# Seven Strassen products in fewer PSUM banks: sums kept in PSUM, copied out by ScalarE on the way

## The chip, the cores and the metric

The kernel runs on one core of one Trainium2 chip. The metric is the device time of one execution in microseconds (us); the time before is the median of three runs. A trace of one profiled execution shows every instruction of the five engines: PE is TensorE's matmul, PEld its weight load, DVE is VectorE, ACT is ScalarE, POOL is GpSimd, and SP issues most of the transfers.

## The reference

One layer of an encoder on 512 tokens with a model width of 2048, in float32. After an RMS norm one input projection makes, for each of three branches (A, B, C) with four heads of 128 columns, the columns q, k, v and a gate, and besides them three merge gates of 2048 columns. The branches are three kinds of attention. Their outputs are projected up, weighted by the sigmoid of the merge gates, added, and sent through one output projection:

```python
hn = rmsnorm(x, norm_g)
proj = jnp.einsum('bsd,dc->bsc', hn, w_in)
...
up = jnp.einsum('bsnw,nwd->bsnd', ys, w_up)
merged = jnp.sum(gates * up, axis=2)
return x + jnp.einsum('bsd,de->bse', merged, w_out)
```

## The kernel before

**Precision.** Every large product is made from three matmuls in the type float32r: an operand is split into a rounded high part and a remainder, and `mm3` (L100) adds high by high, high by low and low by high in one PSUM tile. The split of a weight tile (`split_to`, L91) is one ACT copy to `wh` and one DVE subtraction to `wl`, 128x1024 elements each.

**Products.** The input projection and the output projection take two column tiles of 128 columns at a time (`pair_task`, L298). Both operands are halved: the weights by the two halves of the model dimension, the tokens into a left half (`LH`, 256 tokens) and a right half (`RH`). Strassen's scheme in Winograd's form then needs seven products instead of eight. Each product is a *unit* (`Unit`, L124): 8 k tiles of three matmuls, so 24 matmuls of 128x256, after which `after_of` (L337) brings the product out of PSUM. With c1 and c2 the two column tiles, the results are

```
c1.L = P1 + P2            U2 = P1 + P6        U3 = U2 + P7
c2.L = U3 - P4            c2.R = U3 + P5      c1.R = U2 + P5 + P3
```

Before the change each product has a PSUM tile of its own from a ring of four (`acc`, L77, and the pool `pa`, L59), and the sums are made in SBUF: ACT copies P1 (L347), and seven DVE additions follow (L349 for P2, L351 for P6, L355 for P7, L359 for P4, L363 and L364 for P5, L368 for P3). The order of the products is 1, 2, 6, 7, 4, 5, 3. There are 54 pairs: 46 in the input projection and 8 in the output projection. The first pair of the output projection has `late=True` and another order (1, 2, 5, 3, 6, 7, 4), since its operands are only just being made. In the seven other pairs of the output projection `before_last` (`rest`, L796) adds the residual input while the last product is still running.

**Order of the work.** `units` is one list: the first head's plain column tiles (`col_task`), then pairs. A head of branch C, B or A takes four pairs: q and k, a pair of merge gates, v and gate, a pair of merge gates (the last head has its two gate pairs at the end). The work of its attention is hung between the units by offsets (`OFF`, L870, and `at`). After the input projection come the up projections (`up_units`, L719) and the output projection. While a unit runs, the weights of the two units after it are split (`LA`; `wh` and `wl` have three buffers each), so the ACT split of a unit waits until PE is done with the unit three before it.

**Who decides the order on an engine.** The program is written in order, and the framework's planner gives each engine its final list by simulating the program: the earliest written instruction that is ready in its simulation goes next. PE's own order is held fixed to the written one for the first 17 units only (L850 to L854); after that the planner may put a later unit's matmuls ahead of an earlier one's. Temporary tiles of 128x512 (`t2`, L68) come from one pool of 21 buffers. They hold the norms and scores of the attention as well as a pair's `u`, `c1` and `c2`. The planner hands the buffers out in the order in which the tiles' first writes are written in the program, so the first write of a pair's `u` (the copy of P1) is listed behind every earlier written first write of such a tile.

## Time and profile before

| | before |
|---|---|
| median of 3 runs | 1399.99 us (1399.92 to 1400.05) |
| profiled execution, first to last instruction | 1397.6 us |
| mean granted TensorE clock | 0.995 |
| busy: PE, PEld | 1366.3 us, 1316.7 us |
| busy: DVE, ACT, POOL | 1191.8 us, 729.7 us, 53.7 us |

The profiled execution has no time beside its span; the runs' median is 2.4 us above that span, which is what lies before the first and after the last instruction. Matmuls are pipelined: a 128x256 matmul is shown as about 0.28 us long while the next one starts 0.12 us after it, so PE's busy time says where PE had work, and the distance of two starts says how fast it went. In a row of the timeline stand the start, the length, engine and line, the operation, output and inputs; in square brackets stands the engine's idle time before it and what ended that.

### The profile page before, as it was taken

Reading aid. Unit: us, or ns where it says so; the run is one execution under the profiler, and the core shown is the slowest. Engines: PE = TensorE matmul, PEld = TensorE weight load, DVE = VectorE, ACT = ScalarE, POOL = GpSimd, SP = SyncE. Lnnn points to the kernel's source line nnn. Section 1 sums busy time; section 2 is a strip of 40 time slices with the busy share of each in tenths; the row PEclk is TensorE's granted clock in tenths of the full one; section 3 lists DMA queues with packets and bytes.
Section 4 is the critical chain, followed back from the end, with each engine's and each line's share of the span. In section 5 each row is a group of like instructions: output and inputs, shape, how many; then the busy total and the mean of one; then the engine's idle time right before and its main releaser. Section 6 shows DMA issues by size and latency. Waiting matters only on the chain.

```text
span 1397.6 us, 25474 instructions
## 1 busy us (share of the span) xinstructions
PE 1366.3 (98%) x10452; PEld 1316.7 (94%) x10452; DVE 1191.8 (85%) x1671; ACT 729.7 (52%) x1042; POOL 53.7 (4%) x60
## 2 busy tenths in 40 slices
PE   6969999999999999999999999999999999999999
PEld 3759999999999999999999999999999988899999
DVE  8999898887978889888888888888888888898886
ACT  6345564544545555555556555545555755453332
POOL 4730000000000000000000000000000000000000
PEclk9989999999999999999999999999999999999999
DMA  7113334323344244342433333333233766535542
GB/s 272 46 46 106 122 102 126 121 91 114 106 129 126 95 114 128 113 129 95 117 122 115 121 94 119 113 114 121 91 115 103 273 197 203 169 109 176 164 151 76
DMA packets 63093, 176.39 MB, mean 126 GB/s; under 512 B 7400, under 2 KB 9320, under 8 KB 62976
## 3 DMA queue, kind: packets, MB, share of 16 engines
q1 hardware_dynamic: 59520, 170.49, 38.4%
q10 hardware_dynamic: 3456, 4.26, 0.8%
q8 instruction: 82, 1.34, 0.4%
q14 instruction: 35, 0.29, 0.1%
HBM read 155.04 MB, written 19.69 MB: 125 GB/s over the span
## 4 chain that ended last, share of the span: by engine, by line
PE 92%; DVE 5%; issue 1%; ACT 0%; POOL 0%; DMA 0%; SPq 0%; DVEq 0%; ACTq 0%; POOLq 0%
PE acc L101 27%; PE acc L103 27%; PE acc L102 27%; PE att L103 3%; PE att L101 3%; PE att L102 3%; DVE x L255 1%; DVE wl L93 1%; PE att L548 1%; PE att L517 1%; PE att L570 1%; DVE x1l L93 1%; PE att L571 1%; PE att L569 1%; DVE t23l L93 0%
## 5 line engine op out<-in xcount | busy, mean ns | idle before, releaser
L92 ACT ACTIVATE wh<-raw 128x1024 fp32r<-128x1024 f32 (+1 forms) x418 | 435.7, 1043 | 549.2 <-PE acc L102 488.2
L93 DVE TENSOR_TENSOR wl<-raw,wh 128x1024 fp32r<-128x1024 f32 (+1 forms) x418 | 503.9, 1206 | 96.7 <-ACT wh L92 95.9
L102 PE MATMUL acc<-x1l,wh 128*128 128x256 f32 (+1 forms) x768 | 222.3, 289 | 10.5 <-DVE x1l L93 10.5
L103 PE MATMUL acc<-x1h,wl 128*128 128x256 f32 (+1 forms) x768 | 222.0, 289 | 2.2 <-DVE wl L93 2.2
L101 PE MATMUL acc<-x1h,wh 128*128 128x256 f32 (+1 forms) x768 | 223.7, 291 | 0.0
L101 PE MATMUL acc<-x2h,wh 128*128 128x256 f32 (+1 forms) x768 | 223.6, 291 | 0.0
L102 PE MATMUL acc<-x2l,wh 128*128 128x256 f32 (+1 forms) x768 | 221.9, 289 | 0.9 <-DVE x2l L93 0.9
L103 PE MATMUL acc<-x2h,wl 128*128 128x256 f32 (+1 forms) x768 | 221.8, 289 | 0.0
L101 PE MATMUL acc<-t23h,wh 128*128 128x256 f32 x736 | 209.7, 285 | 0.0
L103 PE MATMUL acc<-t23h,wl 128*128 128x256 f32 x736 | 208.4, 284 | 0.0
L102 PE MATMUL acc<-t23l,wh 128*128 128x256 f32 x736 | 208.1, 283 | 0.0
L102 PEld LDWEIGHTS acc<-x1l,wh 128*128 128x128 f32 x768 | 147.8, 192 | 13.4 <-DVE x1l L93 11.2
L103 PEld LDWEIGHTS acc<-x1h,wl 128*128 128x128 f32 x768 | 147.8, 193 | 3.9 <-DVE wl L93 2.4
L102 PEld LDWEIGHTS acc<-x2l,wh 128*128 128x128 f32 x768 | 148.0, 193 | 2.4 <-DVE x2l L93 1.1
L101 PEld LDWEIGHTS acc<-x1h,wh 128*128 128x128 f32 x768 | 147.9, 193 | 1.8 <-issue 0.2
L101 PEld LDWEIGHTS acc<-x2h,wh 128*128 128x128 f32 x768 | 148.2, 193 | 1.3
L103 PEld LDWEIGHTS acc<-x2h,wl 128*128 128x128 f32 x768 | 148.0, 193 | 1.3
L101 PEld LDWEIGHTS acc<-t23h,wh 128*128 128x128 f32 x736 | 141.0, 192 | 0.5
L102 PEld LDWEIGHTS acc<-t23l,wh 128*128 128x128 f32 x736 | 141.0, 192 | 0.1
L103 PEld LDWEIGHTS acc<-t23h,wl 128*128 128x128 f32 x736 | 140.7, 191 | 0.3
L101 PE MATMUL acc<-t,wh 128*128 128x256 f32 x368 | 105.1, 286 | 0.0
L102 PE MATMUL acc<-t,wh 128*128 128x256 f32 x368 | 104.4, 284 | 0.0
(256 smaller groups left out, 2728.0 us busy)
## 6 DMA issues: line engine op xcount, KB each, us to landing
raw<-in_w_col SPq DMA_DIRECT2D x192, 512.0 KB, 3.6
raw<-in_w_out SPq DMA_DIRECT2D x32, 512.0 KB, 3.8
gl<-c SPq DMA_DIRECT2D x48, 256.0 KB, 2.0
raw<-in_w_up SPq DMA_DIRECT2D x32, 384.0 KB, 3.2
sg<-gl SPq DMA_DIRECT2D x48, 256.0 KB, 5.0
x<-in_xT SPq DMA_DIRECT2D x16, 256.0 KB, 5.4
xr<-in_xT SPq DMA_DIRECT2D x16, 256.0 KB, 4.4
yd<-y SPq DMA_DIRECT2D x11, 256.0 KB, 2.0
```

What stands on the lines that cost most here:

```text
L92: nc.scalar.activation(hi, src, AF.Copy)
L93: nc.vector.tensor_sub(lo, src, f(hi))
L101: nc.tensor.matmul(ps, lh, rh, start=start, stop=False)
L102: nc.tensor.matmul(ps, lh, rl, start=False, stop=False)
L103: nc.tensor.matmul(ps, ll, rh, start=False, stop=stop)
L255: nc.vector.scalar_tensor_tensor(x, x, gn[:, kt:kt + 1], rstd[0], op0=ALU.mult, op1=ALU.mult)
L517: nc.tensor.transpose(ps[:, blk(i)], st["p"][i][:, blk(j)], identf)
L548: nc.tensor.matmul(ps[:, i * P:], nu_r if i == j else nones_r, part, start=i == j and part is st["lk"][j][0], stop=False)
L569: nc.tensor.matmul(o, vh[:, blk(j)], st["h"][j], start=j == 0, stop=False)
L570: nc.tensor.matmul(o, vl[:, blk(j)], st["h"][j], start=False, stop=False)
L571: nc.tensor.matmul(o, vh[:, blk(j)], st["l"][j], start=False, stop=j == QB - 1)
```

## The change

Products are now accumulated onto each other in PSUM. A pair uses three tiles: bank 0 takes P1, P6, P7 and P4 on top of each other, bank 2 takes P5 and P3, bank 1 takes P2. Between two products of a bank the sum so far is copied or read: ACT copies P1, then U2 = P1 + P6, then P5; DVE adds U3 (standing in bank 0) to c2.R and U2 to what stands in bank 2. P4 enters with the other sign, for which the fourth operand is formed the other way round (`combos`, `merged_combos`), so that the last sum in bank 0 is c2.L itself and ACT copies it out. The order of the products is 1, 2, 6, 5, 7, 3, 4. The late pair keeps its order and its additions.

The PSUM ring of four becomes two buffers for bank 0 and one each for banks 1 and 2; the plain column tiles of the first head and the up projections take tiles from the same three. In the output projection the residual is added to c1 and to the right half of c2 after P3, and the left half of c2 is made by one DVE addition of the residual onto bank 0 after P4, so the last store is c2's left half instead of c1's right half. Per pair of the input projection there are three DVE additions instead of seven and four ACT copies instead of one; a pair of the output projection has three ACT copies.

```diff
-    def acc():
-        return pa.tile([P, S], F32, tag="acc", name=nm("acc"))
+    def acc(i=0):
+        return pa.tile([P, S], F32, tag=f"acc{i}", name=nm("acc"), bufs=1 if i else 2)
...
-    def mm3(ps, lh, ll, rh, rl, start, stop):
+    def mm3(ps, lh, ll, rh, rl, start, stop, more=False):
+        nc.tensor.matmul(ps, lh, rh, start=start, stop=False, skip_group_check=more)
...
-        nc.gpsimd.tensor_sub(u[:, LH], t[:, LH], b[:, LH])
+        nc.gpsimd.tensor_sub(u[:, LH], b[:, LH], t[:, LH])
...
-        order = (1, 2, 5, 3, 6, 7, 4) if late else (1, 2, 6, 7, 4, 5, 3)
+        order = (1, 2, 5, 3, 6, 7, 4) if late else (1, 2, 6, 5, 7, 3, 4)
...
         def mms_of(i):
+            p = order[i]
+            bank = i % 4 if late else {2: 1, 5: 2, 3: 2}.get(p, 0)
+            more = not late and p in (6, 7, 4, 3)
+
             def go(u):
-                st["ps"] = ps = acc()[:, LH]
+                if not more:
+                    st[bank % 3] = acc(bank % 3)[:, LH]
+                st["ps", p] = ps = st[bank % 3]
                 for j in range(UK):
-                    mm3(ps, u.hi[:, j, :], u.lo[:, j, :], *ops[order[i]](j), j == 0, j == UK - 1)
+                    mm3(ps, u.hi[:, j, :], u.lo[:, j, :], *ops[p](j), j == 0 and not more, j == UK - 1, more)
             return go
...
                 if p == 1:
                     nc.scalar.activation(u[:, LH], ps, AF.Copy)
                 elif p == 2:
                     add(c1[:, LH], u[:, LH], ps)
+                elif p == 5:
+                    nc.scalar.activation(c2[:, RH], ps, AF.Copy)
+                elif not late:
+                    if p == 6:
+                        nc.scalar.activation(u[:, RH], ps, AF.Copy)
+                    elif p == 7:
+                        add(c2[:, RH], c2[:, RH], ps)
+                    elif p == 3:
+                        add(c1[:, RH], u[:, RH], ps)
+                    elif before_last is not None:
+                        add(c2[:, LH], st["r"][:, LH], ps)
+                    else:
+                        nc.scalar.activation(c2[:, LH], ps, AF.Copy)
...
-        c = {r: col_task(col(n, r, h), xs, scaled(st, r)) for r in (Q, K, V, G)}
+        c = {r: col_task(col(n, r, h), xs, scaled(st, r), max(0, r - 1)) for r in (Q, K, V, G)}
...
-        nc.vector.tensor_sub(u, t[:, LH], b[:, LH])
+        nc.vector.tensor_sub(u, b[:, LH], t[:, LH])
...
-        def rest(c1l, c1r, c2, e=e):
-            for c, i, sl in ((c2, 1, slice(0, S)), (c1l, 0, LH), (c1r, 0, RH)):
-                if i == 1 or sl is LH:
-                    r = t2("xr")
-                    nc.sync.dma_start(r, xT[e + i])
+        def rest(c1, c2r, e=e):
+            for c, i, sl in ((c1, 0, slice(0, S)), (c2r, 1, RH)):
+                r = t2("xr")
+                nc.sync.dma_start(r, xT[e + i])
                 nc.vector.tensor_add(c, c, r[:, sl])
-            nc.scalar.dma_start(out[e + 1], c2)
-            nc.scalar.dma_start(out[e][:, LH], c1l)
+            nc.scalar.dma_start(out[e], c1)
+            nc.scalar.dma_start(out[e + 1][:, RH], c2r)
+            return r
...
-            nc.scalar.dma_start(out[e][:, RH], c1[:, RH])
+            nc.scalar.dma_start(out[e + 1][:, LH], c2[:, LH])
```

More of the change, by code (lines that the diff above doesn't have):

```diff
@@ L98, in split @@
         return hi, lo
-    def mm3(ps, lh, ll, rh, rl, start, stop):
-        nc.tensor.matmul(ps, lh, rh, start=start, stop=False)
-        nc.tensor.matmul(ps, lh, rl, start=False, stop=False)
-        nc.tensor.matmul(ps, ll, rh, start=False, stop=stop)
+    def mm3(ps, lh, ll, rh, rl, start, stop, more=False):
+        nc.tensor.matmul(ps, lh, rh, start=start, stop=False, skip_group_check=more)
+        nc.tensor.matmul(ps, lh, rl, start=False, stop=False, skip_group_check=more)
+        nc.tensor.matmul(ps, ll, rh, start=False, stop=stop, skip_group_check=more)
     nc.scalar.preload_act_table_set("natural_log_exp_and_others")
@@ L282, in halves, with col_task @@
         return [w_col[c, 0], w_col[c, 1]]
-    def col_task(srcs, xs, evac):
-        ps = Lazy(acc)
+    def col_task(srcs, xs, evac, bank=0):
+        ps = Lazy(lambda: acc(bank))
         def mms(i):
@@ L340, in go @@
             def go():
-                ps = st["ps"]
+                ps = st["ps", p]
                 if i == 0:
@@ L344, in go @@
                 u, c1, c2 = st["u"], st["c1"], st["c2"]
-                add, sub = nc.vector.tensor_add, nc.vector.tensor_sub
+                add = nc.vector.tensor_add
                 if p == 1:
@@ L349, in go @@
                     add(c1[:, LH], u[:, LH], ps)
+                elif p == 5:
[11 more added lines that the diff above has]
+                        nc.scalar.activation(c2[:, LH], ps, AF.Copy)
                 elif p == 6:
                     add(u[:, LH], u[:, LH], ps)
-                    if late:
-                        add(c1[:, RH], c1[:, RH], u[:, LH])
+                    add(c1[:, RH], c1[:, RH], u[:, LH])
                 elif p == 7:
                     add(u[:, RH], u[:, LH], ps)
-                    if late:
-                        add(c2[:, RH], c2[:, RH], u[:, RH])
+                    add(c2[:, RH], c2[:, RH], u[:, RH])
                 elif p == 4:
-                    sub(c2[:, LH], u[:, RH], ps)
-                elif p == 5 and late:
-                    nc.scalar.activation(c2[:, RH], ps, AF.Copy)
-                elif p == 5:
-                    add(c2[:, RH], u[:, RH], ps)
-                    add(u[:, LH], u[:, LH], ps)
-                elif late:
+                    add(c2[:, LH], u[:, RH], ps)
+                else:
                     add(c1[:, RH], c2[:, RH], ps)
-                else:
-                    add(c1[:, RH], u[:, LH], ps)
                 if i == 5 and before_last is not None:
-                    before_last(c1[:, LH], u[:, LH], c2)
+                    st["r"] = before_last(c1, c2[:, RH])
                 if i == 6:
```

## The prediction

> **What bounds the kernel now.** I read the page first, then the busy time by stage, then PE's waits, and then the timelines of single engines around the steps that change. The page has the totals:

> ```profile
> span 1397.6 us, 25474 instructions
> PE 1366.3 (98%) x10452; PEld 1316.7 (94%) x10452; DVE 1191.8 (85%) x1671; ACT 729.7 (52%) x1042; POOL 53.7 (4%) x60
> ```

> By stage (columns: stretch, its length, then busy time and instruction count of PE, PEld, DVE, ACT and POOL, then PE's granted clock, DMA share, GB/s):

> ```profile
> 0.00:35.00 35.00, 22.58 (x65) 12.27 (x66) 30.74 (x48) 21.38 (x33) 14.01 (x25) 1.00 0.74 272
> 35.00:100.00 65.00, 51.38 (x251) 42.21 (x250) 62.78 (x78) 28.18 (x46) 38.17 (x32) 0.89 0.15 43
> 100.00:200.00 100.00, 100.00 (x823) 99.44 (x822) 89.38 (x141) 53.94 (x85) 0.00 (x0) 1.00 0.37 114
> 200.00:1060.00 860.00, 860.00 (x7079) 854.62 (x7078) 731.25 (x1007) 463.13 (x655) 1.51 (x3) 1.00 0.37 113
> 1060.00:1150.00 90.00, 90.00 (x547) 80.59 (x546) 73.68 (x116) 56.40 (x89) 0.00 (x0) 1.00 0.61 204
> 1150.00:1250.00 100.00, 98.87 (x509) 84.70 (x507) 85.03 (x133) 54.92 (x81) 0.00 (x0) 1.00 0.52 171
> ```

> From 100 to 1150 us PE has work in every moment, 1050 of 1050 us. Its 31.3 us without work (1397.6 less 1366.3) lie elsewhere: 12.4 before 35 us, 13.6 up to 100 us, 1.1 in the stage before the output projection, the rest after it. Inside the busy stretch PE runs at one pace; here the last product of a group, four short attention matmuls, the next product:

> ```profile
> 453.04 0.28 PE L101 MATMUL acc<-t23h,wh 128*128 128x256 f32 x1
> 453.16 0.28 PE L102 MATMUL acc<-t23l,wh 128*128 128x256 f32 x1
> 453.28 0.28 PE L103 MATMUL acc<-t23h,wl 128*128 128x256 f32 x1
> 453.40 0.81 PE L101 MATMUL att<-qkh,qkh 128*128 128x128 f32 x4
> 454.04 0.28 PE L101 MATMUL acc<-t,wh 128*128 128x256 f32 x1
> ```

> One start every 0.12 us, so a unit of 24 is 2.88 us. The change leaves the matmuls as they are, so over 1050 us it can take nothing away; it can only put gaps in.

> **What is removed.** The additions and the copy that exist now:

> ```profile
> L349 DVE TENSOR_TENSOR c<-u,acc 128x256 f32<-128x256 f32 x54 | 22.6, 419 | 27.0 <-PE acc L103 26.7 <-issue 0.3
> L364 DVE TENSOR_TENSOR u<-u,acc 128x256 f32<-128x256 f32 x53 | 22.0, 414 | 0.0
> L347 ACT ACTIVATE u<-acc 128x256 f32<-128x256 f32 x54 | 19.8, 366 | 5.5 <-PE acc L103 5.5
> ```

> Four additions of about 0.415 us go in each of the 46 pairs of the input projection and in 7 of the output projection: 53 x 4 x 0.415 = 88 us off DVE, to about 1104 us (one of the four in an output pair is a residual addition, of the same size). ACT gets three copies in 46 pairs and two in 7, 152 x 0.366 = 56 us, to about 785 us. On the path neither counts: DVE's work is hidden behind PE's 1050 us, and ACT stays far from full. Would DVE's relief help where DVE does hold PE up, before 100 us? The first addition of a pair runs only at

> ```profile
> 96.18 0.40 DVE L349 TENSOR_TENSOR c<-u,acc 128x256 f32<-128x256 f32 x1
> ```

> so in the 62.78 busy us of that stage there is nothing to remove: 0 us. The sign change of the fourth operand swaps two inputs of one subtraction, 0 us. At the end the last product is followed by one DVE addition and one store of half a tile, as now: 0 us. The weight buffers of a pair are let go one each after the units 3, 5 and 6 and two after unit 4, counted from 0, before and after; so the loads on SP's queue keep their times.

> **What is added.** PE now waits inside a pair. P6 goes onto P1's bank, so it needs ACT's copy of P1; P7 needs the copy of U2; P3 the copy of P5; P4 DVE's addition. In the written order one product, 2.88 us, lies between each sum and the next product of its bank. At an ordinary place that is enough, as in the last pair, where P6's first matmul is the one on m23h:

> ```profile
> 1378.03 0.36 ACT L347 ACTIVATE u<-acc 128x256 f32<-128x256 f32 x1
> 1379.80 0.28 PE L101 MATMUL acc<-m23h,wh 128*128 128x256 f32 x1
> ```

> The copy ends 1.4 us before P6. The copies of U2 and P5 stand the same way behind one weight split, and I put them at nothing; without that cover each would cost its lateness as below.

> There are 13 pairs where it is not enough: the second gate pair (121 us) and the pair after it, and the v-and-gate pairs of the heads whose attention starts just before. There `u` must wait its turn among the temporary tiles, behind the scores (C) or the second norm (B, A). In the first of eight pairs of B and A, ACT and DVE run:

> ```profile
> 444.84 1.06 ACT L92 ACTIVATE wh<-raw 128x1024 fp32r<-128x1024 f32 x1 [0.64 <-PE acc L102]
> 447.72 1.06 ACT L92 ACTIVATE wh<-raw 128x1024 fp32r<-128x1024 f32 x1 [1.82 <-PE acc L102]
> 450.60 1.06 ACT L92 ACTIVATE wh<-raw 128x1024 fp32r<-128x1024 f32 x1 [1.82 <-PE acc L102]
> 451.56 0.61 ACT L92 ACTIVATE qkh<-rs 128x512 fp32r<-128x512 f32 x1
> 452.08 0.37 ACT L347 ACTIVATE u<-acc 128x256 f32<-128x256 f32 x1
> 447.64 0.28 PE L101 MATMUL acc<-t23h,wh 128*128 128x256 f32 x1
> 1062.84 0.37 ACT L347 ACTIVATE u<-acc 128x256 f32<-128x256 f32 x1
> 1058.40 0.28 PE L101 MATMUL acc<-t23h,wh 128*128 128x256 f32 x1
> ```
> ```profile
> 442.32 0.41 DVE L359 TENSOR_TENSOR c<-u,acc 128x256 f32<-128x256 f32 x1
> 442.99 0.41 DVE L364 TENSOR_TENSOR u<-u,acc 128x256 f32<-128x256 f32 x1
> 445.59 0.41 DVE L368 TENSOR_TENSOR c<-u,acc 128x256 f32<-128x256 f32 x1
> 445.92 0.69 DVE L239 TENSOR_TENSOR rw<-rw,rv 128x512 f32<-128x512 f32 x1
> 446.52 1.22 DVE L93 TENSOR_TENSOR wl<-raw,wh 128x1024 fp32r<-128x1024 f32 x1
> 447.66 0.69 DVE L240 SCALAR_TENSOR_TENSOR rs<-rw,rt 128x512 f32<-128x512 f32 x1
> ```

> P6 begins at 447.64, the copy ends at 452.45: P6 would be 4.81 us late; the last two ACT and PE rows are the eighth such pair, late by the same. In the three pairs of C and the two early ones:

> ```profile
> 272.95 0.28 PE L101 MATMUL acc<-t23h,wh 128*128 128x256 f32 x1
> 277.87 0.37 ACT L347 ACTIVATE u<-acc 128x256 f32<-128x256 f32 x1
> 117.42 0.28 PE L101 MATMUL acc<-t23h,wh 128*128 128x256 f32 x1
> 121.33 0.36 ACT L347 ACTIVATE u<-acc 128x256 f32<-128x256 f32 x1
> 141.03 0.28 PE L101 MATMUL acc<-t23h,wh 128*128 128x256 f32 x1
> 144.95 0.37 ACT L347 ACTIVATE u<-acc 128x256 f32<-128x256 f32 x1
> ```

> 5.29 us in each C pair, 4.27 and 4.29 us in the early ones. Together 8 x 4.81 + 3 x 5.29 + 4.27 + 4.29 = 62.9 us.

> Two things take from that. First, the planner may let P5, whose bank is free, go ahead of a blocked P6 (all 13 pairs lie behind the 17 units with a fixed order). That is 2.88 us more cover: 1.93 us remain at each of eight, 2.41 at each of three, 1.39 and 1.41: 25.5 us. Second, DVE has fewer additions ahead of the norm: L359, L363, L364 and L368 shrink to one of them, about 1.0 us at their distance of 0.33 us. In B and A, by estimate, L239 then starts at 444.9 and L240 comes ahead of the `wl` split that now separates them, another 1.14 us. 2.1 us is more than 1.93, so I put these eight at 0; in C I take 1.0 us off, leaving 1.41; the early two I leave whole. Sum: 0 + 3 x 1.41 + 1.39 + 1.41 = 7.0 us. The ends are 0 us (the relief reaches C too and the early ones by chance) and 25.5 us (none of it arrives, since the new copies fill ACT's free time). What queues behind the new wait on PE is everything: later products and the attention's matmuls, whose scores need the same norm.

> So 1397.6 + 7.0 is a span of 1404.6 us, and with the 2.4 us by which the median of 1399.99 lies above this span, **1407 us**.

> [...]

> **The rivals.** *All covered.* The relief and P5's going ahead hide all 13 places. For it: ordinary places have 1.4 us to spare, and 2.1 us of relief against 1.93. Against it: PE's list is fixed in a simulated run, and 13 places must each fit. Time: 1400 us, within 2.8. *Order kept.* P5 does not go ahead and each P6 waits in place: 62.9 us, 1463 us. Such gaps may also cost clock. PE's longest waits are two in the stage from 35 to 100 us:

> ```profile
> PE acc L102 <- DVE x1l L93: 10.5, 2, 6.3
> ```

> That stage's clock is 0.89 over 65 us, 7.2 us lost, 3.6 us for each of the two waits; 13 x 3.6 is 47 us more, about 1510 us. Against it: PE already takes attention matmuls between products, out of the written order. [...] *Faster.* Where the up projections hand over to the output projection, PE lacks 1.1 us of work before 1250 and waits on splits; fewer additions in the next pair let these come sooner. It decides if no other place stalls: at most 3 us, 1397 us. That the sums would not come about at all would change no time: the matmuls and waits are the same.

> **How the numbers follow.** The forecast, partial stalls of 3 to 25.5 us: 0.44. All covered: 0.38. Order kept: 0.08. Faster: 0.10. A measurement of this kernel can tell 0.2%, 2.8 us, from no change. So slower 0.44 + 0.08 = 0.52, same 0.38, faster 0.10. The forecast's own range is 1403 to 1426 us. With the covered case and the faster one the range is 1397 to 1426 us; outside are the kept order and a little of the faster case.

> **What would show it.** In the changed kernel: DVE busy near 1104 us and ACT near 785 us; PE's waits name ACT's copy of P1 (L347 now) at up to 13 places of 1 to 2 us, in the C pairs and before 150 us above all; PE's busy time between 100 and 1060 us falls short of the stretch by the same sum; in those pairs matmuls on x1h (P5) come ahead of t23h (P6). Wrong would be: no such waits at all (covered); waits over 4 us with a lower clock (kept order); a gain inside 100 to 1150 us, which would mean that PE's pace of 0.12 us depends on the other engines' traffic; or waits at ordinary pairs, which would mean that ACT's copies come later than the 1.4 us to spare.

## The result, and the profile after

The changed kernel is slower: 1473.8 us (median of four runs, 1473.0 to 1475.2) against 1400.0 us beside it, a ratio of 1.052 (95% interval 1.051 to 1.054). The prediction was 1407 us with a range of 1397 to 1426; the sign was right, the size was far off. The profiled execution spans 1472.4 us (before 1397.6), with a mean TensorE clock of 0.977 (before 0.995). The totals:

```profile
PE 1392.8 (95%) x10452; PEld 1337.6 (91%) x10452; DVE 1132.2 (77%) x1459; ACT 768.9 (52%) x1194; POOL 53.8 (4%) x60
```

PE has the same 10452 instructions, DVE 212 fewer, ACT 152 more, as predicted in number. Those of PE's waits that the kernel before does not have on these tiles (columns: total us, times, longest us):

```profile
PE att L103 <- ACT qkh L93: 35.7, 8, 4.5
...
PE att L564 <- ACT lkh L93: 6.1, 3, 2.0
...
PE acc L103 <- ACT u L366: 4.1, 9, 1.3
...
PE acc L103 <- ACT u L359: 1.3, 1, 1.3
```

The first two rows name the attention, the norm's result `qkh` and C's `lkh`, and not the copy of P1 (L359 now). That is because of what stands next in PE's list: a wait is put down to what the next matmul in the list needs. The first of the eight v-and-gate pairs of B and A, with the end of the gate pair before it:

```profile
440.99 0.28 PE L103 MATMUL acc<-x1h,wh 128*128 128x256 f32 x1
...
443.83 0.28 PE L103 MATMUL acc<-t23h,wh 128*128 128x256 f32 x1
...
446.71 0.28 PE L103 MATMUL acc<-x1h,wh 128*128 128x256 f32 x1
...
448.18 0.39 PE L103 MATMUL acc<-t23h,wh 128*128 128x256 f32 x1 [0.35 <-ACT u L366]
...
456.91 0.28 PE L103 MATMUL acc<-x1h,wh 128*128 128x256 f32 x1
...
459.79 0.28 PE L103 MATMUL acc<-x2h,wh 128*128 128x256 f32 x1
...
462.67 0.28 PE L103 MATMUL acc<-x1h,wh 128*128 128x256 f32 x1
...
465.19 0.28 PE L103 MATMUL acc<-x1h,wh 128*128 128x256 f32 x1
...
470.16 1.54 PE L103 MATMUL att<-qkh,qkh 128*128 128x128 f32 x4 [4.46 <-ACT qkh L93]
471.50 0.41 PE L103 MATMUL acc<-t23h,wh 128*128 128x256 f32 x1
```

From 456.91 on: P1, P2, then P5, which did go ahead of P6; then 4.62 us more than the usual 0.12 between two starts, four scores, and P6 at 471.50. ACT in the same stretch:

```profile
449.23 0.69 ACT L237 ACTIVATE rt<-att,epsc 128x512 f32<-128x512 f32 x1
...
461.14 0.63 ACT L93 ACTIVATE qkh<-rs 128x512 fp32r<-128x512 f32 x1
...
463.77 0.67 ACT L237 ACTIVATE rt<-att,epsc 128x512 f32<-128x512 f32 x1
...
469.48 0.63 ACT L93 ACTIVATE qkh<-rs 128x512 fp32r<-128x512 f32 x1 [2.34 <-DVE rs L486]
470.02 0.37 ACT L359 ACTIVATE u<-acc 128x256 f32<-128x256 f32 x1
470.28 0.38 ACT L363 ACTIVATE c<-acc 128x256 f32<-128x256 f32 x1
```

P1 was done at about 459.8. Its copy runs at 470.02, at once behind the second norm's last ACT step: the turn among the temporary tiles, as the prediction read it. It ends 13.5 us after P1's start. Before the change P1 of this pair started at 441.88 and its copy ended at 452.45, 10.6 us after that:

```profile
441.88 0.28 PE L101 MATMUL acc<-x1h,wh 128*128 128x256 f32 x1
```

The norm has become longer: the first of the two takes 11.9 us here, from `rt` at 449.23 to `qkh` at 461.14. Before the change it took 6.2 us:

```profile
433.85 0.67 ACT L235 ACTIVATE rt<-att,epsc 128x512 f32<-128x512 f32 x1
...
440.04 0.61 ACT L92 ACTIVATE qkh<-rs 128x512 fp32r<-128x512 f32 x1
```

DVE shows why:

```profile
442.16 1.23 DVE L94 TENSOR_TENSOR wl<-raw,wh 128x1024 fp32r<-128x1024 f32 x1 [0.48 <-ACT wh L93]
447.89 2.44 DVE L94 TENSOR_TENSOR wl<-raw,wh 128x1024 fp32r<-128x1024 f32 x2 [4.50 <-ACT wh L93]
450.25 1.22 DVE L321 TENSOR_TENSOR raw<-raw,raw 128x1024 f32<-128x1024 f32 x1
451.42 0.42 DVE L368 TENSOR_TENSOR c<-c,acc 128x256 f32<-128x256 f32 x1
451.75 1.22 DVE L330 TENSOR_TENSOR raw<-raw,raw 128x1024 f32<-128x1024 f32 x1
452.89 1.22 DVE L94 TENSOR_TENSOR wl<-raw,wh 128x1024 fp32r<-128x1024 f32 x1
454.02 0.68 DVE L241 TENSOR_TENSOR rw<-rw,rv 128x512 f32<-128x512 f32 x1
```

In the gate pair the planner set P6 inside P5: 18 of P5's matmuls from 440.99, all of P6 from 443.83, P5's last six from 446.71. So no product ends, and no weight buffer comes free, for 5.7 us; DVE stands idle for 4.50 us, and the splits it could not make then fall into the norm.

**The account.** From the starts of PE's matmuls (a pause is a start over 0.4 us later than usual), behind 100 us: eight pauses of 4.62 us, 36.9; three of 2.18 us in the C pairs, 6.6; eight of 0.52 us in the gate pairs, where P7 waits for the copy of U2, 4.1; and two in the second gate pair, 1.46 us where P6 waits for P1's copy (at 123 us) and 1.49 us where P7 waits for U2's (at 128 us). That is 50.5 us; the pauses around the output projection are 0.5 us shorter than before. Then there is the clock. PEclk is the last column but two, PE's busy time the second figure; the 4.62 us pause lies in the first two rows:

```profile
463.29:466.71 3.42, 2.42 (x21) 2.21 (x19) 1.70 (x2) 3.39 (x6) 0.00 (x0) 1.00 0.75 186
466.71:470.12 3.41, 0.00 (x0) 0.00 (x0) 3.38 (x5) 1.07 (x3) 0.00 (x0) 1.00 0.56 202
470.12:473.53 3.41, 3.37 (x14) 3.27 (x15) 2.59 (x5) 0.54 (x2) 0.00 (x0) 0.50 0.00 0
473.53:476.95 3.42, 3.42 (x31) 3.42 (x31) 0.96 (x4) 1.60 (x4) 0.00 (x0) 1.00 0.00 0
```

Behind each of the eight pauses, and behind two of the three in C, TensorE runs at half clock for 3.41 or 6.83 us. Before the change there is none between 105 us and the last two microseconds. In the stretches at half clock after the change, 54.6 us in all, the matmuls that follow each other without a pause lose 21.7 us against their usual distances. 50.0 and 21.7 are 71.7 of the 74.8 us by which the span grew; 1.2 us were lost in the first 100 us, and 1.9 us, in smaller delays, I have not placed.

### The profile page after: what moved, and what is told of

Its sections match the earlier page's. It is cut to its first block, busy times and chain, and to the rows that moved or that the text cites. A ratio compares the mean times of both kernels' runs of the same rounds, so it can differ in the third digit from the quotient of the medians.

```text
span 1472.4 us, 25408 instructions
## 1 busy us (share of the span) xinstructions
PE 1392.8 (95%) x10452; PEld 1337.6 (91%) x10452; DVE 1132.2 (77%) x1459; ACT 768.9 (52%) x1194; POOL 53.8 (4%) x60
## 4 chain that ended last, share of the span: by engine, by line
PE 86%; DVE 7%; ACT 4%; issue 3%; DMA 1%; POOL 0%; SPq 0%; ACTq 0%; DVEq 0%; POOLq 0%
PE acc L103 25%; PE acc L104 25%; PE acc L105 24%; PE att L103 3%; PE att L105 2%; PE att L104 2%; ACT wh L93 1%; DVE wl L94 1%; DVE x L257 1%; PE att L564 1%; PE att L533 1%; PE att L587 1%; DVE x1l L94 1%; PE att L586 0%; PE att L585 0%
## 5 line engine op out<-in xcount | busy, mean ns | idle before, releaser
L93 ACT ACTIVATE wh<-raw 128x1024 fp32r<-128x1024 f32 (+1 forms) x418 | 435.1, 1042 | 553.1 <-PE acc L104 504.6
L104 PE MATMUL acc<-x1l,wh 128*128 128x256 f32 (+1 forms) x768 | 222.3, 289 | 10.6 <-DVE x1l L94 10.5
L103 PE MATMUL acc<-x1h,wh 128*128 128x256 f32 (+1 forms) x768 | 223.5, 291 | 0.0
L103 PE MATMUL acc<-x2h,wh 128*128 128x256 f32 (+1 forms) x768 | 223.3, 291 | 0.0
L103 PE MATMUL acc<-t23h,wh 128*128 128x256 f32 x736 | 217.9, 296 | 5.4 <-ACT u L366 4.1
L104 PE MATMUL acc<-t23l,wh 128*128 128x256 f32 x736 | 215.6, 293 | 0.0
L105 PE MATMUL acc<-t23h,wl 128*128 128x256 f32 x736 | 214.9, 292 | 0.0
L103 PEld LDWEIGHTS acc<-t23h,wh 128*128 128x128 f32 x736 | 149.0, 202 | 8.8 <-ACT u L366 6.9
L103 PEld LDWEIGHTS acc<-x1h,wh 128*128 128x128 f32 x768 | 147.7, 192 | 2.0 <-issue 0.2
L104 PEld LDWEIGHTS acc<-t23l,wh 128*128 128x128 f32 x736 | 148.5, 202 | 1.1
L103 PEld LDWEIGHTS acc<-x2h,wh 128*128 128x128 f32 x768 | 148.2, 193 | 1.4
L105 PEld LDWEIGHTS acc<-t23h,wl 128*128 128x128 f32 x736 | 148.2, 201 | 0.0
L103 PE MATMUL acc<-t,wh 128*128 128x256 f32 x368 | 104.6, 284 | 0.0
L105 PE MATMUL acc<-t,wl 128*128 128x256 f32 x368 | 104.1, 283 | 0.0
```

Of the source, the lines that this page charges most:

```text
L93: nc.scalar.activation(hi, src, AF.Copy)
L103: nc.tensor.matmul(ps, lh, rh, start=start, stop=False, skip_group_check=more)
L104: nc.tensor.matmul(ps, lh, rl, start=False, stop=False, skip_group_check=more)
L105: nc.tensor.matmul(ps, ll, rh, start=False, stop=stop, skip_group_check=more)
```

## The experiments

Theory 1: a product that is added onto a bank waits for the copy of that bank's last sum; the copy is late because it waits for its turn behind the norm; long waits then cost clock. Rivals: ScalarE's added copies delay the norm (theory 2); the new order and the planner cost the time without any sharing of banks (theory 3), with a special form, that the planner's weaving of two products makes the norm late (3a).

**Every product in a bank of its own.** Order and sign of the change stay; of ACT's copies only those of P1 and P5 do, and DVE adds the rest in SBUF again.

```diff
-        return pa.tile([P, S], F32, tag=f"acc{i}", name=nm("acc"), bufs=1 if i else 2)
+        return pa.tile([P, S], F32, tag="acc", name=nm("acc"))
...
-            more = not late and p in (6, 7, 4, 3)
+            more = False
...
```

> The new order of the products, the new sign of T4 and the copies of P1, P5 stay, but every product gets a bank of its own from a ring of four, and VectorE adds the sums in SBUF; so nothing is added up in PSUM. Theory 1 (a product that goes onto a bank whose last sum has not been copied out waits for that copy, and TensorE's clock halves after the longest of these waits): the 24 gaps of 53 us and the half-clock stretches go, 1400 us within 5. Theory 2 (ScalarE's new copies delay the attention's norm): only the copies of P1 and P5 are left, about half of the loss, 1430 to 1440 us. Theory 3 (order, sign and planner alone): the loss stays, 1460 us or more.

1400.1 us, ratio 0.9998 (0.9989 to 1.0007). The copy of P1 is as late as in the kernel before, and nobody minds. ACT, then PE:

```profile
452.22 0.62 ACT L93 ACTIVATE qkh<-rs 128x512 fp32r<-128x512 f32 x1
452.74 0.36 ACT L359 ACTIVATE u<-acc 128x256 f32<-128x256 f32 x1
```
```profile
442.29 0.28 PE L103 MATMUL acc<-x1h,wh 128*128 128x256 f32 x1
...
448.05 0.28 PE L103 MATMUL acc<-t23h,wh 128*128 128x256 f32 x1
```

P6 starts at 448.05, and the copy ends 5.05 us after that, at 453.10. Order and sign alone cost nothing; theory 3 falls in its plain form.

**Only bank 0 shared, only bank 2 shared.**

```diff
...
-            more = not late and p in (6, 7, 4, 3)
+            more = not late and p in (6, 7, 4)
...
```

> P6, P7 and P4 go onto P1's bank as in the change; P5 and P3 get banks of their own, and P3 is added by VectorE. Theory 1 (waits for copies of P1 and U2 on the one bank): gaps of about 4.6 us at eight v-and-gate pairs and 0.5 us at eight gate pairs stay, 1465 to 1475 us. If the bank of P5 and P3 is what costs, 1400 to 1410 us.

1446.6 us, 1.0325 (1.031 to 1.034). The eight pauses are there, seven of 2.46 us and one of 2.70 (19.9 in all), the three of C at 2.2 to 2.4; the 0.5 us at the gate pairs are gone. So bank 0 is what costs, but less than the 1465 us and more that I had said: PE's list came out another, and the norm is less late in it (in the first of the eight pairs the copy ends 8.3 us after the start of P1's last matmul, in the change 10.7).

```diff
...
-            more = not late and p in (6, 7, 4, 3)
+            more = not late and p == 3
...
```

> Only P3 goes onto P5's bank; the other products have banks of their own from a ring of four, and VectorE adds the rest. P3 comes three products (8.6 us) after P5, so P5's copy has 5.8 us in hand even where it is late. Theory 1: no gaps, 1400 us within 3. If any bank that is added onto costs: 1405 us or more.

1401.0 us, 1.0006 (0.9997 to 1.0016), no wait on a copy. The three products between that I had counted on are not there: in 45 of the 46 pairs of the input projection only P7 and a few single matmuls lie between P5 and P3, the copy starts 1.2 to 1.7 us after the start of P5's last matmul, and it is done 1.4 us or more ahead of P3. In the second gate pair the copy comes 8.3 us after P5, and there the planner put P4 and the next pair's P1 in between as well; P3 starts 0.7 us after the copy. So adding onto a bank cost nothing here (1.0006) where other products covered the copy; a late copy with one product between did not occur here.

**P1's copy out of the queue of temporary tiles.** A half tile of its own; the pool of small columns gives up two of its eight buffers to make room.

```diff
...
-                    st["u"], st["c1"], st["c2"] = t2("u"), t2("c1"), t2("c2")
+                    st["c1"], st["c2"] = t2("c1"), t2("c2")
...
+                    st["ul"] = cp.tile([P, HS], F32, tag="ul", name=nm("ul"), bufs=1)
+                elif p == 6 and not late:
+                    st["u"] = t2("u")
...
-                    nc.scalar.activation(u[:, LH], ps, AF.Copy)
+                    nc.scalar.activation(st["ul"], ps, AF.Copy)
...
```

> P1's copy goes into a half tile of its own, outside the temporary tiles, so that it need not wait for its turn behind the norm; U2's copy takes a temporary tile when P6 is done. Banks, sums and order as in the change. Theory 1 with the turn among the temporary tiles as the cause of the late copy: the gaps in front of P6 at eight pairs of B and A (36.9 us), at three of C (6.6 us) and the early two (2.9 us) go, and the half-clock stretches with them (18 us); the 0.5 us at eight gate pairs may stay: 1402 to 1412 us. If the copy is late because ScalarE is busy (theory 2), or if sharing a bank costs in itself, the gaps stay: 1460 us or more.

1408.8 us, 1.0056 (1.0039 to 1.0073). All the pauses of the heads are gone, those of the gate pairs too, and the half clock behind them (the mean clock is 0.992, in the change 0.977). ACT works as long as in the change (772.8 us for 768.9), so theory 2 falls. One pause is left, at 126 us:

```profile
131.84 0.79 PE L571 MATMUL att<-lkh,nu_r 128*128 128x512 f32 x1 [5.60 <-ACT lkh L93]
```
```profile
131.16 0.63 ACT L93 ACTIVATE lkh<-lk 128x512 fp32r<-128x512 f32 x1 [2.35 <-DVE lk L560]
131.70 0.37 ACT L373 ACTIVATE u<-acc 128x256 f32<-128x256 f32 x1
```

It is the same thing once more: U2's copy, which now takes a temporary tile at P6's end, stands behind the tiles of the stick-breaking and comes right after the last of them.

**Both copies out of the queue.** `ul` and `ur`, each a half tile. Room for the second is made in two ways: by taking the tile of the forget gate's weights from the temporary ones and working out a mask from another constant; or, in the second kernel, by that mask and by letting the head's norms use the constant of minus ones.

```diff
...
-                        nc.scalar.activation(u[:, RH], ps, AF.Copy)
+                        nc.scalar.activation(st["ur"], ps, AF.Copy)
...
-                        add(c1[:, RH], u[:, RH], ps)
+                        add(c1[:, RH], st["ur"], ps)
...
```

> Both copies that are sums on their way, P1's and U2's, go into half tiles of their own (their 1 KB each comes from an early tile that is taken from the temporary ones and a mask that is worked out from another constant). Banks and order as in the change. In the kernel with P1's copy alone moved, one gap of 5.8 us was left, at 126 us, where U2's copy stood behind the stick-breaking tiles, and two half-clock windows behind it (3.4 us), 9.2 us in all against 8.7 us of loss. Theory 1: that gap goes too, no wait of TensorE on a copy is left, 1400 us within 2. If the copies cost ScalarE or TensorE something beside the waits: 1403 us or more.

1410.0 us, 1.0071 (1.0059 to 1.0084): a miss. There is no wait on a copy, and no half clock behind 140 us. But the first 100 us got slower: the matmul that starts at 99 us before the change starts 8.6 us later here (in the change 1.2 us later), and the granted clock from 35 to 110 us is 0.82, where the change and the kernel before have 0.91. So the early tile was a bad place to take room from.

> As the kernel with both copies in half tiles of their own, but the second kilobyte comes from a constant of ones (the head's norms use the constant of minus ones, with the sign turned in the scale) and no longer from the early tile, which held up the first 100 us there. That kernel had no wait of TensorE on a copy and no half clock behind 140 us, and lost its 10 us ahead of 140 us. Theory 1 (all of the loss was the waits and the clock behind them): 1400 us within 2. If the sums in PSUM cost something beside the waits, 1403 us or more; if the 57 us that VectorE is relieved of were worth anything to this kernel, 1397 us or less.

1402.1 us, 1.0013 (1.0004 to 1.0021), just outside the 1400 within 2 that I gave, and at the edge of what can be told from no change. Its totals, and its stage from 400 to 1100 us:

```profile
PE 1366.8 (98%) x10452; PEld 1316.8 (94%) x10452; DVE 1128.8 (81%) x1458; ACT 770.9 (55%) x1196; POOL 54.1 (4%) x59
```
```profile
400.00:1100.00 700.00, 700.00 (x5756) 695.24 (x5755) 557.78 (x698) 411.90 (x651) 1.57 (x3) 1.00 0.37 118
```

All sums stand in PSUM and all of ACT's copies are made, and PE works 700 of 700 us at full clock, as before the change. All but 2 us of the loss was waits on the copies and the clock behind them. Two pauses that the kernel before does not have, 1.19 us at 126 us and 1.15 us at 128 us, stand in front of a product whose weights are not split yet. And 63 us less of DVE work, 1128.8 us busy for 1191.8, brought nothing.

**P5 written ahead of P6.**

```diff
-        order = (1, 2, 5, 3, 6, 7, 4) if late else (1, 2, 6, 5, 7, 3, 4)
+        order = (1, 2, 5, 3, 6, 7, 4) if late else (1, 2, 5, 6, 7, 3, 4)
```

> P5 is written ahead of P6 (order 1, 2, 5, 6, 7, 3, 4); the rest is as in the change. The planner put P5 ahead already, but in the gate pairs it wove P5's and P6's matmuls together, so that two of three weight buffers were held for 5.7 us and VectorE's work bunched up in the norm's time. If that weaving is what makes the norm late (theory 3a), the 0.5 us gaps at the gate pairs go and the 4.6 us gaps at the v-and-gate pairs shrink below 2 us: 1405 to 1430 us. If the norm is late for other reasons, the 4.6 us gaps stay: 1465 to 1475 us.

1456.7 us, 1.040 (1.038 to 1.042), between the two cases that I had given, so a miss: 3.77 us at the eight pairs, nothing at the gate pairs there. The planner no longer sets P6 inside P5, but makes other swaps (P3 ahead of P7, the next pair's P1 ahead of P4). 17 us of the 74 went.

**The norm written two units earlier, and four later.**

```diff
-OFF = dict(cs=4, ct=12, nk=5, nq=4, s=12, t=16, v=1, av=8, a0=11, b0=18, c0=3, c1=2, man=17, last=3, l1=0, l2=0)
+OFF = dict(cs=4, ct=12, nk=3, nq=2, s=12, t=16, v=1, av=8, a0=11, b0=18, c0=3, c1=2, man=17, last=3, l1=0, l2=0)
```

> The change with the two norms of a head of B and A written two units (5.8 us) earlier, at the second and third unit behind the pair in place of the fourth and fifth; nothing else. Theory 1 (P1's copy waits for its turn behind the norm's tiles): the norm is done 5.8 us sooner, which is more than the 4.6 us gap, so the eight gaps of 4.6 us go, and the half-clock windows behind them; the C pairs, the early two and the gate pairs keep theirs: 1472.4 - 36.9 - 14 = about 1420 us, 1410 to 1430. If the norm's place does not set the copy's time, 1470 us.

1468.5 us, 1.049 (1.047 to 1.051): a miss. The pauses of 4.62 us are gone, but four or five, mostly of 0.7 to 1.4 us, stand in their place in each head, most of them on the weight splits (15.7 us in all on `wh`, 13.4 us on `wl`). P6 still sits inside P5, and, as I read the trace, the two weight buffers that come free late now fall together with the norm's ACT and DVE work.

> The change with the two norms written four units later, behind the v-and-gate pair's P1 and P2, so that P1's tile now comes ahead of the norm's tiles in the order of the temporary tiles, while the scores stay where they were. Theory 1: P6 no longer waits for P1's copy; the gap in front of P6 goes or moves to the scores, which now follow the norm closely; 1405 to 1450 us, and no row in which TensorE waits for P1's copy or for the norm inside the first three products. If it is the lateness of the norm alone (and not the order) that costs: worse than the change, over 1480 us.

This is the line above with nq=8, nk=9. 1453.0 us, 1.038 (1.037 to 1.040), just outside what I gave. P1's copy is now on time (at 460.63 for a product that started at 456.64), since its tile comes ahead of the norm's. But P5's copy goes into `c2`, whose first write now stands behind the second norm:

```profile
477.22 0.63 ACT L93 ACTIVATE qkh<-rs 128x512 fp32r<-128x512 f32 x1 [4.25 <-DVE rs L486]
477.75 0.37 ACT L363 ACTIVATE c<-acc 128x256 f32<-128x256 f32 x1
```

P3 needs it, so the planner put a product of the next pair ahead, whose weights were not split yet. The queue of tiles had only been handed to the next copy.

> The norms written four units later, as in the kernel that came out at 1453 us, and P5 written ahead of P6. There P1's copy no longer came late, but the planner wove P5's and P6's matmuls together, held two of three weight buffers, and the next weights' splits fell into the norm: 2.7 us in front of P7's partner and 1.05 us in front of the scores at each of up to eight heads. If the weaving is the cause of that second loss, it goes with P5 ahead, and the 0.5 us at the gate pairs too: the C pairs' 6 us, the early 3 us and some half clock remain, 1407 to 1425 us. If the norm's work alone makes the splits late, the gaps stay: 1445 us or more.

Both edits together. 1443.3 us, 1.0305 (1.029 to 1.032): a miss. The waits for weights shrink, but P7 now follows P6 directly and waits 1.72 us at each of the eight pairs for U2's copy, and the scores wait 0.5 to 2 us for the norm.

**TensorE's order held as written.** This takes the planner's swaps out; `man` is the unit at which the hold ends. First the control, the kernel before:

```diff
+    order.close()
     assert not side, side
...
-OFF = dict(cs=4, ct=12, nk=5, nq=4, s=12, t=16, v=1, av=8, a0=11, b0=18, c0=3, c1=2, man=17, last=3, l1=0, l2=0)
+OFF = dict(cs=4, ct=12, nk=5, nq=4, s=12, t=16, v=1, av=8, a0=11, b0=18, c0=3, c1=2, man=1000000, last=3, l1=0, l2=0)
```

> The kernel before with TensorE's order held as written to the end, attention matmuls included; only the other engines' order is planned. It is the control for the next kernel. The attention's matmuls can no longer slip behind a product when their input is late: 1400 us if nothing waits there, more if they do, up to 1440 us (twelve attention heads of about 3 us).

1423.3 us, 1.0166 (1.0151 to 1.0181). Four pauses of 2.95 us stand in front of the transposes of B and one of 2.97 us in the output projection, with half clock behind four of the five (the mean clock is 0.989, in the kernel before 0.995). P1's copy is as late as in the kernel before: in the first of the eight pairs P6 starts at 453.11 and the copy ends at 457.91, 4.80 us after that. Then the change:

> The change with TensorE's order held as written to the end. P5 can't go ahead of P6, and no two products are woven together. If the copy of P1 is late by what the trace of before shows (4.81 us at eight pairs, 5.29 at three, 4.27 and 4.29 early), the gaps come to 62.9 us over the control, and to about 80 us with the half clock behind them. If weaving is what made the norm later in the change by 2.9 us, the copy ends here 10.6 to 11 us after P1's start in the v-and-gate pairs, as in the kernel before, and not 13.5 us; then the gaps are 4.6 to 5.2 us in spite of P5's staying behind. If the norm is late for another reason, the gaps are 7.7 us, and the whole over 100 us above the control.

1466.4 us, 1.047 (1.045 to 1.049), 43 us above the control, at a mean clock of 0.978. PE's first row of waits, one of the eight places, and ACT there:

```profile
PE acc L103 <- ACT u L359: 33.0, 12, 5.2
```
```profile
472.84 0.28 PE L103 MATMUL acc<-x1h,wh 128*128 128x256 f32 x1
...
480.58 0.38 PE L103 MATMUL acc<-t23h,wh 128*128 128x256 f32 x1 [1.82 <-ACT u L359]
```
```profile
480.16 0.36 ACT L359 ACTIVATE u<-acc 128x256 f32<-128x256 f32 x1
```

Now the wait is put down to the copy itself, at 12 places: eight of 1.98 us, three in C of 5.33 us, and an early one of 3.13 us. The prediction had read lateness of 4.81, 5.29 and 4.27 us. In B and A the copy is 2.83 us earlier than that. So much DVE's relief was to give (I had put it at 2.1), though no run takes the additions away by themselves. In C there is none. I had expected 4.6 us or more here. P1 of this pair started at 472.84, so the copy ends 7.7 us after it; with the order held the copy comes earlier than before the change, not later.

**The order held, P5 ahead.** Both edits, so that P5 covers P6 with nothing set inside it.

> TensorE's order held as written, with P5 written ahead of P6 (1, 2, 5, 6, 7, 3, 4): what the prediction thought the planner would do, without weaving. With the order held and P6 third, the gaps in front of P6 were 1.98 us at eight pairs of B and A, 5.33 us at three of C and 3.13 us early. If P5's going ahead is by itself 2.88 us of cover and the weaving is what made the norm late in the change: 0 at the eight, 2.4 to 2.5 us at the three, about 0.3 us early. P7 then stands right behind P6 and waits for U2's copy, with no product between: 0.5 to 1 us at most of the 24 pairs, more where the copy stands behind the norm. In all 1425 to 1455 us. If P5's place itself makes the norm late, the eight gaps in front of P6 are 4 us or more, and the time over 1465 us.

1492.3 us, 1.065 (1.064 to 1.067), slower than I gave, but for one reason that stands in its first row of waits:

```profile
PE acc L103 <- ACT u L366: 63.2, 53, 1.4
```

In front of P6 no pair of a head waits any more. In B and A the copy ends 7.7 us after P1's start, as with P6 third, and three products, 8.64 us, now lie ahead of P6. In C, where I expected 2.4 us, the copy ends 8.1 us after P1's start, with P6 third 11.0 us. I put that down to PE's waits in front of P7, which leave the scores' work more time; so the C pairs do not test the cover. In front of P7, which follows P6 at once, 1.0 to 1.5 us go in nearly every pair: a copy with no product to cover it cost 1.46 us here, for 0.37 us of ACT work. That it is so many pairs, the output projection's too, makes the total.

## Why the prediction was wrong

**What held.** PE bounds the middle, where before the change it works 1050 of 1050 us, and DVE's relief was worth nothing there: 1402 us with the copies of P1 and U2 out of the queue. The list of places was nearly right: the pauses stand in the eight pairs of B and A, the three of C and the first of the two early ones. The second early pair does not wait (its copy ends at 143.77, P6 starts at 146.46), and the pauses in front of P7 were not on the list. The cause at each place was right, the turn among the temporary tiles, shown by moving one copy (74 us of loss become 9). That the sharing of a bank makes the lateness cost is shown by the same copy coming as late without harm where every product has a bank of its own (5.05 us late, and 1400.1 us). The lateness itself was read well: 5.33 us against 5.29 in C with the order held.

**The step that failed** is "I put these eight at 0". Its terms were 4.81 us of lateness, less 2.88 us for P5's going ahead, less 2.1 us of relief. Each term holds by itself in B and A with the order held: the lateness is read rightly and 2.8 us come off it (4.80 becomes 1.98), and with P5 ahead nothing is left. They do not add up in the planner's list. The planner let P5 go ahead, and in the gate pair set P6 inside it; with other swaps this changed when weight buffers come free, the splits bunched, and the copy came 2.9 us later than before instead of 2.1 us earlier: 4.81 + 2.9 - 2.88 is the 4.8 us that PE is late, of which 4.62 us are one pause. 36.9 us came from a term set to 0. The held order shows that the planner's list makes the norm late. That the held weight buffers do it is read from the trace; no run changes them alone. P6's place inside P5 is not enough by itself: in the kernel with P1's copy moved, P6 sits inside P5 too, but behind two of its matmuls and not behind 18. A product then ends after 3.1 us and not after 5.7, DVE idles for 1.90 us and not for 4.50, and the second norm's last ACT step ends 10.5 us after P1's start, where it ended 10.3 us after it before the change and 13.2 us in the change. Nor is that place needed: the kernel with P5 written first keeps 3.77 of 4.62 us without it. So how much of the 2.9 us belongs to P6's place stays open.

**Sizes.** In C I took 1.0 us of relief off 2.41; 2.18 us were measured, so the relief hardly reached C. Of the early two the first came out at 1.46 us for 1.39, the second at nothing for 1.41. The copies of U2, put at nothing, cost 1.49 us at the first early pair, where P7 follows P6 at once, and 0.52 us at eight gate pairs, 4.1 us, where only six matmuls of P5 and one of the norm lie between P6 and P7. DVE fell by 59.6 us and ACT rose by 39.2, for 88 and 56 predicted, with the counts as predicted: 212 additions at 0.28 us and 152 copies at 0.26, since neighbours on an engine overlap in the trace (in DVE's rows above one starts at 451.42 with a length of 0.42, the next at 451.75) and the length of a row counts that overlap twice. The plain sums of the lengths fell by 84.8 and rose by 56.9 us.

**The clock** I charged to one rival only. At 21.7 us it is over a quarter of the loss. That rival, *order kept*, gave 1463 us of gaps and 1510 us with the clock; the kernel with the order held is 43 us above its control and came to 1466 us. The change landed between the two figures and showed that rival's sign, waits over 4 us with a lower clock, but by another way: its order was not kept, since P5 did go ahead.

## What to carry to other kernels

Adding onto a buffer in place turned a copy that nobody waited for into a wait of the bounding engine here (1473.8 us, with a bank for each product 1400.1), so look up when such a copy really runs, not when it could: its destination tile stood in a queue behind unrelated work, and a kilobyte of its own for each of two copies took all but 2 us of the loss away. Where a planner rewrites the engine's list, cover found on paper is no term to subtract with full weight; price the case in which its swaps move the work that feeds the wait. And cost a pause of the matmul engine with the clock behind it: here each of the eight pauses of 4.62 us was followed by 3.41 or 6.83 us at half clock.

## What the runs showed of the clock

| PE's pause, share of the window | windows | next window at half clock |
|---|---|---|
| under 0.5 | 238 | 0 |
| 0.5 to 0.6 | 33 | 16 |
| over 0.6 | 43 | 43 |

A second slow window came behind all 14 slow windows that themselves held pauses for 0.17 of their length or more, and behind none of the 45 with 0.15 or less. So the length of a pause did not decide by itself in these traces. A pause of 1.98 us that lay in one window, 0.58 of it, was followed by half clock (five of eight such places with the order held); one of 2.46 us that straddled two windows was not. The kernel with the order held and P5 ahead has 64 pauses, 86 us in all, and one stretch of half clock between 100 us and its end, after the single pause of 3.0 us.
